# Building the second column half of the first matmul from seven half-size products, with operand sums made by accumulating DMA

## The chip, the cores and the metric

The kernel runs on one core of one Trainium2 chip. The metric is the device time of one execution in microseconds (us). A run more than 1.5% above the fastest of its kernel counts as slow and is left out of ratios. The profile is one execution; its span is about 1.8 us shorter than the measured time of the same execution (before: 122.1 against 123.87).

## The reference

```python
m, k, n, p = 1024, 1024, 2048, 1024
h = a @ b                                   # float32, random normal inputs
h = 0.5*h*(1 + tanh(sqrt(2/pi)*(h + 0.044715*h**3)))
return h @ c
```

## The kernel before

Tiles hold h transposed: the first matmul puts 128 columns of b (stationary) against 512 rows of a (moving), sums over eight k tiles in one PSUM bank, and ScalarE writes the GELU. All 16 column tiles are done for the upper 512 rows of a, then for the lower 512.

```python
def mm1(t, h):
    p = ppool.tile([128, H], F32, name="ps")
    for k in range(KT):                                  # 8 matmuls
        nc.tensor.matmul(p, bt(k, t), aT[h][:, k, :], start=(k == 0), stop=(k == KT - 1))
    gelu(t, h, p)
# ... (upper rows, loads, transposes of a's lower rows)
for t in range(NT):                                      # lower rows
    mm1(t, 1)
    # ... sums of c and of h on VectorE, a few per tile
```

The second matmul is already built from seven products of half-size blocks instead of eight (the Winograd form). VectorE makes every sum that this needs:

```python
# t1 = c12 - c11;  t2 = c22 - t1;  t3 = c22 - c12;  s1 = h21 + h22;  s2 = s1 - h11;  s3 = h11 - h21
for j in R: p = bank(); prod(p, whole(h11), whole(c11), j); nc.scalar.activation(u2[j], p, AF.Copy)
for j in range(3): p = bank(); prod(p, whole(h12), whole(c21), j); combine(j, 0, p, u2[j])
# ... then s2 x t2, s3 x t3, s1 x t1, s2 x c22, h22 x t2, each four output tiles of eight matmuls,
#     s2 and t2 having been replaced by s4 = h12 - s2 and t4 = t2 - c21, and one last narrow tile
```

bf16 holds a, b and half of the operands; sums are float32r. Loads that cast go through GpSimd's DMA queue, plain ones and the stores through SyncE's.

Of the kernel before, what the change touches and what calls it, by code (L numbers as in the profile page):

```python
# [19 lines left out]
def kernel(ctx, tc, a, b, c, out):  # L20
    nc = tc.nc
# [8 lines left out]
    W0 = N0 * 128  # L30
    N1 = 4
    W1 = N1 * 128

# [9 lines left out]
    b0stage = ctx.enter_context(tc.tile_pool(name="b0stage", bufs=8))  # L43
# [9 lines left out]
    NH = NT // 2  # L53
    aT = [keep.tile([128, KT, H], BF16, name=f"aT{h}", tag=f"A{h}") for h in range(2)]
    WB = W0 + W1
    b_lo = keep.tile([128, KT, WB], BF16, name="b_lo", tag="B0")
    b_hi = keep.tile([128, KT, N - WB], BF16, name="b_hi", tag="B1")

    def bcols(k0, kn, n0, w):
        if n0 < WB:  # L60
            return b_lo[:, k0:k0 + kn, ds(n0, w)]
        return b_hi[:, k0:k0 + kn, ds(n0 - WB, w)]

    def bt(k, t):
        return bcols(k, 1, t * 128, 128)[:, 0, :]


    hq = [[keep.tile([128, NH, H], F32R if h else BF16, name=f"h{h}{g}") for g in range(2)]
          for h in range(2)]
# [19 lines left out]
    for mt in range(4):  # L89
        load_a0(mt, 2 if mt == 3 else 1)  # L90
# [38 lines left out]
    for mt in range(4):  # L129
        if mt < 3:  # L130
            ab.append(cast_a0(mt + 1))
        turn0(mt, ab[mt], (0,) if mt == 3 else (0, 1))
        if mt < 3:
            warm_up(3)
    cast_b0(0)
    for k in range(KT):
        if k + 1 < KT:
            cast_b0(k + 1)
        for t in range(N0):
            nc.tensor.matmul(ps[t], bt(k, t), aT[0][:, k, :],  # L140
                             start=(k == 0), stop=(k == KT - 1))
# [3 lines left out]
    def gelu(t, h, p):  # L145
        nc.scalar.activation(hq[h][t // NH][:, t % NH, :], p, AF.Gelu_apprx_tanh)  # L146

    for t in range(N0):
        gelu(t, 0, ps[t])


    def load_b(k0, kn, n0, w):
        nc.gpsimd.dma_start(out=bcols(k0, kn, n0, w), in_=bv[:, k0:k0 + kn, ds(n0, w)])

    ps = [(tpool if t < 2 else ppool).tile([128, H], F32, name="pt" if t < 2 else "ps")
          for t in range(N1)]
    for k in range(0, KT, 4):
        load_b(k, 4, W0, W1)
        for i in range(4):
            for t in range(N1):  # L160
                nc.tensor.matmul(ps[t], bt(k + i, N0 + t), aT[0][:, k + i, :],  # L161
                                 start=(k + i == 0), stop=(k + i == KT - 1))
    for t in range(N1):
        gelu(N0 + t, 0, ps[t])


    def mm1(t, h):
        p = ppool.tile([128, H], F32, name="ps")
        for k in range(KT):
            nc.tensor.matmul(p, bt(k, t), aT[h][:, k, :],  # L170
                             start=(k == 0), stop=(k == KT - 1))
        gelu(t, h, p)

    W2 = 384
    for n0 in range(W0 + W1, N, W2):
        for k in range(0, KT, 4):
            load_b(k, 4, n0, W2)

    a1 = []
    for j in range(4):  # L180
        st = abf.tile([128, K], BF16, name="ab1")
        nc.gpsimd.dma_start(out=st, in_=av[:, 4 + j, :])
        a1.append(st)

    def turn(j):
        ab = a1[j]
        pt = tpool.tile([128, KT, 128], BF16, name="pt")
        for k in range(KT):
            nc.tensor.transpose(pt[:, k, :], ab[:, ts(k, 128)], ident)  # L189
        nc.vector.tensor_copy(aT[1][:, :, ts(j, 128)], pt)  # L190

    for t in range(N0 + N1, NT):
        mm1(t, 0)
        if t == NT - 3:
            turn(0)
        if t == NT - 2:
            turn(1)
            turn(2)
            turn(3)
# [7 lines left out]
    (h11, h12), (h21, h22) = hq  # L207
    c11 = keep.tile([128, NH, H], BF16, name="c11")
    c21 = keep.tile([128, NH, H], BF16, name="c21")
    c22 = keep.tile([128, NH, H], F32R, name="c22")  # L210
    c12 = keep.tile([128, NH, H], BF16, name="c12", tag="A0")
# [5 lines left out]
    load_c(c11, 0, 0)  # L217
    load_c(c22, 1, 1)
    load_c(c21, 1, 0)
    load_c(c12, 0, 1)  # L220

    t1 = [astage.tile([128, 2, H], F32R, name="t1", tag="a_st") for _ in range(4)]
# [150 lines left out]
```

## Time and profile before

| | before |
|---|---|
| time, median | 123.75 us (123.52 to 124.07) |
| span of the profile | 122.1 us |
| TensorE busy, VectorE busy | 116.1 us (95%), 64.6 us (53%) |
| chain that ended last | TensorE 88%, DMA 6% |
| second matmul starts, last matmul starts | 68.9 us, 119.0 us |

The page's strip chart has one digit for each fortieth of the span (9 is 90% or more). A line of the chain or of a timeline begins with start and length in us. The lines themselves are in the prediction below.

### The profile page before, as it was taken

To read this page: it belongs to the slowest core of one execution; us is meant where nothing else is said; L and a number is where in the kernel's file an instruction comes from. 1 tells how busy PE (TensorE), PEld (TensorE's weight loads), DVE (VectorE), ACT (ScalarE), POOL (GpSimd) and SP (SyncE) were. 2 spreads that over 40 slices of the span, in tenths; PEclk is the share of its full clock that TensorE was granted. 3 is DMA by queue.
4 is the path that set the end of the run, shared out by engine and by line. 5 is a ranking of instruction groups with operands and counts; after the bars stand their busy time and mean duration, and the time that the engine had idled before them with its cause. 6 is when DMAs were issued, how large, how long until landed. Compare 5 with 4: busy or idle time off the path is not lost.

```text
span 122.1 us, 1486 instructions
## 1 busy us (share of the span) xinstructions
PE 116.1 (95%) x577; PEld 68.3 (56%) x577; DVE 64.6 (53%) x95; ACT 30.7 (25%) x54; POOL 21.5 (18%) x26
## 2 busy tenths in 40 slices
PE   6977999999998999999999999999999999999990
PEld 2542444444456444444444444468888888888880
DVE  0352340000014200006999999999769999974351
ACT  4454752806331133233323331100000000000000
POOL 2000099132440220000000000797000000000000
PEclk9999999999999999999999999999999999999999
DMA  3999969999999999995000000000600022445425
GB/s 144 351 328 347 413 188 191 198 200 205 209 207 206 329 394 231 206 206 97 0 0 0 5 0 3 3 0 0 258 0 0 5 86 86 157 167 191 163 99 167
DMA packets 12582, 18.44 MB, mean 151 GB/s; under 512 B 800, under 2 KB 7584, under 8 KB 12576
## 3 DMA queue, kind: packets, MB, share of 16 engines
q0 software_dynamic: 7968, 8.91, 39.6%
q1 hardware_dynamic: 4464, 9.37, 20.9%
q10 hardware_dynamic: 144, 0.07, 0.2%
q8 instruction: 4, 0.07, 0.2%
q14 instruction: 2, 0.02, 0.0%
HBM read 20.97 MB, written 4.19 MB: 206 GB/s over the span
## 4 chain that ended last, share of the span: by engine, by line
PE 88%; DMA 6%; SPq 2%; DVE 1%; ACT 0%; issue 0%
PE ps L273 41%; PE ps L170 31%; PE ps L140 8%; DMA b_st<-in_b_dram 6%; PE ps L161 3%; PE pt L161 3%; SPq L78 2%; PE pt L189 1%; DVE aT L190 1%; ACT b_lo L126 0%; SPq L85 0%; DVE ot L342 0%; PE pt L115 0%
## 5 line engine op out<-in xcount | busy, mean ns | idle before, releaser
L146 ACT ACTIVATE h<-ps 128x512 fp32r<-128x512 f32 (+1 forms) x30 | 17.3, 602 | 28.6 <-PE ps L170 26.3
L170 PE MATMUL ps<-aT,b_hi 128*128 128x512 bf16 x96 | 21.4, 379 | 0.0
L170 PE MATMUL ps<-aT,b_lo 128*128 128x512 bf16 x80 | 17.4, 379 | 0.0
L170 PEld LDWEIGHTS <-b_hi 128*128 128x128 bf16 x96 | 9.3, 98 | 10.8
L273 PE MATMUL ps<-t,s 128*128 128x512 f32 x64 | 15.0, 392 | 0.0
L273 PE MATMUL ps<-t,h 128*128 128x512 f32 x64 | 14.8, 389 | 0.0
L273 PE MATMUL ps<-c,h 128*128 128x512 bf16 (+2 forms) x80 | 14.2, 336 | 0.0
L313 POOL COPY lk<-u 128x512 f32<-128x512 f32 x1 | 7.7, 7684 | 33.6 <-ACT u L306 33.6
L273 PEld LDWEIGHTS ps<-t,s 128*128 128x128 f32 x64 | 12.0, 188 | 2.6
L273 PEld LDWEIGHTS ps<-t,h 128*128 128x128 f32 x64 | 12.0, 188 | 2.5
L170 PEld LDWEIGHTS <-b_lo 128*128 128x128 bf16 x80 | 7.8, 98 | 9.4
L227 DVE TENSOR_TENSOR t<-c,c 128x1024 fp32r<-128x1024 bf16 x4 | 4.7, 1222 | 15.8 <-DMA c<-in_c_dram 15.7
L190 DVE COPY aT<-pt 128x1024 bf16<-128x1024 bf16 x4 | 2.7, 689 | 19.4 <-PE pt L189 19.3
L140 PE MATMUL ps<-aT,b_lo 128*128 128x512 bf16 x48 | 10.9, 380 | 0.8 <-DVE b_lo L125 0.8
L273 PEld LDWEIGHTS <-h 128*128 128x128 bf16 x80 | 7.2, 98 | 7.0 <-issue 0.3
L140 PEld LDWEIGHTS <-b_lo 128*128 128x128 bf16 x48 | 4.5, 98 | 6.6 <-DVE b_lo L125 1.1
L215 POOL DMA_DIRECT2D c<-in_c_dram x8 | 5.9, 744 | 11.7 <-PE ps L170 6.0
L296 DVE TENSOR_TENSOR ot<-ps,u 128x512 f32<-128x512 f32 x11 | 7.3, 684 | 1.1 <-PE ps L273 1.1
L101 PE MATMUL ps<-warm 128*128 128x512 bf16 x17 | 6.3, 516 | 1.2 <-DVE warm L49 1.2
L273 PE MATMUL ps<-c,s 128*128 128x512 f32 x32 | 7.4, 389 | 0.0
L273 PEld LDWEIGHTS ps<-c,s 128*128 128x128 f32 x32 | 6.0, 188 | 1.2
L125 DVE CAST b_lo<-b_st 128x384 bf16<-128x384 f32 x8 | 2.9, 368 | 5.1 <-DMA b_st<-in_b_dram 5.1
(40 smaller groups left out, 96.5 us busy)
## 6 DMA issues: line engine op xcount, KB each, us to landing
out_dram<-ot SPq DMA_DIRECT2D x15, 256.0 KB, 2.0
c<-in_c_dram POOLq DMA_DIRECT2D x6, 512.0 KB, 14.8
b_st<-in_b_dram SPq DMA_DIRECT2D x7, 384.0 KB, 8.1
c<-in_c_dram POOLq DMA_DIRECT2D x2, 1024.0 KB, 15.0
a_st<-in_a_dram SPq DMA_DIRECT2D x3, 512.0 KB, 4.1
b_hi<-in_b_dram POOLq DMA_DIRECT2D x4, 384.0 KB, 11.3
b_lo<-in_b_dram POOLq DMA_DIRECT2D x2, 512.0 KB, 7.2
ab<-in_a_dram POOLq DMA_DIRECT2D x4, 256.0 KB, 13.9
```

Source lines behind the costliest of these rows:

```text
L101: nc.tensor.matmul(ps[N0 - 1], warm[:, 0:128], warm, start=True, stop=True)
L125: nc.vector.tensor_copy(b_lo[:, k, 0:HW], b_st[k][:, 0:HW])
L140: nc.tensor.matmul(ps[t], bt(k, t), aT[0][:, k, :], start=(k == 0), stop=(k == KT - 1))
L146: nc.scalar.activation(hq[h][t // NH][:, t % NH, :], p, AF.Gelu_apprx_tanh)
L161: nc.tensor.matmul(ps[t], bt(k + i, N0 + t), aT[0][:, k + i, :], start=(k + i == 0), stop=(k + i == KT - 1))
L170: nc.tensor.matmul(p, bt(k, t), aT[h][:, k, :], start=(k == 0), stop=(k == KT - 1))
L190: nc.vector.tensor_copy(aT[1][:, :, ts(j, 128)], pt)
L215: nc.gpsimd.dma_start(out=dst[:, t:t + 4, :], in_=cv[:, r * NH + t:r * NH + t + 4, ts(q, H)])
L227: nc.vector.tensor_tensor(t1[i], c12[:, ts(i, 2), :], c11[:, ts(i, 2), :], op=SUB)
L273: nc.tensor.matmul(p, lhs(t)[:, ts(j, 128)], rhs(t)[:, q], start=(t == 0), stop=(t == NH - 1))
L296: nc.vector.tensor_tensor(ot, u if swap else p, p if swap else u, op=op)
L313: nc.gpsimd.tensor_copy(last_keep, last)
```

## The change

Output columns 1024 to 2047 of the first matmul (half of its 256 matmuls) become a two-by-two block product in the same seven-product form: 112 matmuls for 128. Its sums come on top of those that fill VectorE in the second matmul, so several, old and new, are made by accumulating DMA instead: the buffer holds a first term (for t2 and t3 ScalarE writes it there), and a transfer from GpSimd's queue adds the second. The core of the diff, with cuts marked by dots and the comments added here:

```diff
-    for t in range(N0 + N1, NT):
-        mm1(t, 0)
...
+    mm1(6, 0, h11[:, 6, :])
+    turn(0)
+    mm1(7, 0, h11[:, 7, :])
+    for j in (1, 2, 3):
+        turn(j)
... (as1, as2, as3, bt3, b12 in place, bt2: twelve sums on VectorE)
+    for t in range(NH):
+        mm1(t, 1, h21[:, t, :])
... (loads of c11, c12, c22)
+    for j in R:  # product 1, bf16
+        p = bank()
+        prod(p, KH, whole(bx), whole(aT[0]), j)
+        nc.scalar.activation(v2[:, j, :], p, AF.Copy)
+    for j in R:  # product 2, bf16
+        p = bank()
+        prod(p, KH, whole(bx, KH), whole(aT[0], KH), j)
+        add_gelu(h12[:, j, :], p, v2[:, j, :])
...
+    for j in R:  # product 3, float32r as all below
+        p = bank()
+        prod(p, KH, pairs(bt2), pairs(as2), j)
+        tt(v2[:, j, :], p, v2[:, j, :], op=ADD)
...
+    for i in range(2):
+        nc.gpsimd.dma_start(out=as2[i], in_=aT[0][:, P2[i + 2], :], accum_op=ADD)
+    for i in range(2):
+        nc.gpsimd.dma_start(out=bt2[i], in_=bx[:, P2[i + 2], :], accum_op=ADD)
... (product 4, bt3 and as3; product 5, b12 and as1)
+    c21 = keep.tile([128, NH, H], BF16, name="c21", tag="BX")
     load_c(c21, 1, 0)
...
+    for i in R:
+        nc.scalar.mul(t2[i], c22[:, P2[i], :], -1.0)
+        nc.gpsimd.dma_start(out=t2[i], in_=t1[:, P2[i], :], accum_op=ADD)
... (product 6, b22 and as2; product 7, bt2 and a22; s1 and s2 on VectorE; h11 x c11)
+    for i in R:
+        nc.scalar.mul(t3p(i), c12[:, P2[i], :], -1.0)
+        nc.gpsimd.dma_start(out=t3p(i), in_=c22[:, P2[i], :], accum_op=ADD)
... (h12 x c21, s3 on VectorE, s2 x t2)
-        sum_s4(i)
-        sum_t4(2 * j)
-        sum_t4(2 * j + 1)
+    for g in range(2):
+        nc.gpsimd.dma_start(out=s2[g], in_=h12[:, ts(g, KH), :], accum_op=ADD)
+    for i in R:
+        nc.gpsimd.dma_start(out=t2[i], in_=c21[:, P2[i], :], accum_op=ADD)
... (s3 x t3, s1 x t1, s2 x c22, h22 x t2, the narrow tile)
```

Line numbers in the profiles of the changed kernels are those of the changed files: L167 is `mm1`, L220 is `prod`, L285 the accumulates of t2, L339 and L340 t3's scaled copies and accumulates.

More of the change, by code (lines that the diff above doesn't have):

```diff
@@ L29 @@
     N0 = 6
-    W0 = N0 * 128
-    N1 = 4
-    W1 = N1 * 128
+    W0 = N // 2
+    KH = KT // 2
+    NH = NT // 2
+    R = range(4)
     av = a.rearrange("(mt p) k -> p mt k", p=128)
@@ L42 @@
     abf = ctx.enter_context(tc.tile_pool(name="abf", bufs=4))
-    b0stage = ctx.enter_context(tc.tile_pool(name="b0stage", bufs=8))
+    b0stage = ctx.enter_context(tc.tile_pool(name="b0stage", bufs=6))
     opool = ctx.enter_context(tc.tile_pool(name="opool", bufs=4))
@@ L51 @@
     make_identity(nc, ident)
-    NH = NT // 2
     aT = [keep.tile([128, KT, H], BF16, name=f"aT{h}", tag=f"A{h}") for h in range(2)]
-    WB = W0 + W1
-    b_lo = keep.tile([128, KT, WB], BF16, name="b_lo", tag="B0")
-    b_hi = keep.tile([128, KT, N - WB], BF16, name="b_hi", tag="B1")
-    def bcols(k0, kn, n0, w):
-        if n0 < WB:
-            return b_lo[:, k0:k0 + kn, ds(n0, w)]
-        return b_hi[:, k0:k0 + kn, ds(n0 - WB, w)]
-    def bt(k, t):
-        return bcols(k, 1, t * 128, 128)[:, 0, :]
-    hq = [[keep.tile([128, NH, H], F32R if h else BF16, name=f"h{h}{g}") for g in range(2)]
-          for h in range(2)]
+    a22 = keep.tile([128, KH, H], F32R, name="a22", tag="A22")
+    b_lo = keep.tile([128, KT, W0], BF16, name="b_lo", tag="B0")
+    bx = keep.tile([128, KT, H], BF16, name="bx", tag="BX")
+    b12 = keep.tile([128, KH, H], F32R, name="b12", tag="BT")
+    b22 = keep.tile([128, KH, H], F32R, name="b22", tag="BR")
+    (h11, h12), (h21, h22) = [[keep.tile([128, NH, H], F32R if h else BF16, name=f"h{h}{g}")
+                               for g in range(2)] for h in range(2)]
     a_st, b_st = {}, {}
@@ L88 @@
     gate = consts.tile([128, 1], F32, name="gate")
-    for mt in range(4):
+    for mt in R:
         load_a0(mt, 2 if mt == 3 else 1)
@@ L128 @@
     ab = [cast_a0(0)]
-    for mt in range(4):
+    for mt in R:
         if mt < 3:
@@ L139 @@
         for t in range(N0):
-            nc.tensor.matmul(ps[t], bt(k, t), aT[0][:, k, :],
+            nc.tensor.matmul(ps[t], b_lo[:, k, ts(t, 128)], aT[0][:, k, :],
                              start=(k == 0), stop=(k == KT - 1))
@@ L143, with gelu, bank @@
             turn0(3, ab[3], (1,))
-    def gelu(t, h, p):
-        nc.scalar.activation(hq[h][t // NH][:, t % NH, :], p, AF.Gelu_apprx_tanh)
+    def gelu(dst, src):
+        nc.scalar.activation(dst, src, AF.Gelu_apprx_tanh)
+    def bank(w=H):
+        return ppool.tile([128, w], F32, name="ps", padded_shape=[128, H])
     for t in range(N0):
-        gelu(t, 0, ps[t])
-    def load_b(k0, kn, n0, w):
-        nc.gpsimd.dma_start(out=bcols(k0, kn, n0, w), in_=bv[:, k0:k0 + kn, ds(n0, w)])
-    ps = [(tpool if t < 2 else ppool).tile([128, H], F32, name="pt" if t < 2 else "ps")
-          for t in range(N1)]
-    for k in range(0, KT, 4):
-        load_b(k, 4, W0, W1)
-        for i in range(4):
-            for t in range(N1):
-                nc.tensor.matmul(ps[t], bt(k + i, N0 + t), aT[0][:, k + i, :],
-                                 start=(k + i == 0), stop=(k + i == KT - 1))
-    for t in range(N1):
-        gelu(N0 + t, 0, ps[t])
-    def mm1(t, h):
-        p = ppool.tile([128, H], F32, name="ps")
-        for k in range(KT):
-            nc.tensor.matmul(p, bt(k, t), aT[h][:, k, :],
-                             start=(k == 0), stop=(k == KT - 1))
-        gelu(t, h, p)
-    W2 = 384
-    for n0 in range(W0 + W1, N, W2):
-        for k in range(0, KT, 4):
-            load_b(k, 4, n0, W2)
+        gelu(h11[:, t, :], ps[t])
     a1 = []
-    for j in range(4):
+    for j in R:
         st = abf.tile([128, K], BF16, name="ab1")
@@ L183 @@
         a1.append(st)
+    nc.gpsimd.dma_start(out=b12, in_=bv[:, 0:KH, W0 + H:N])
+    nc.gpsimd.dma_start(out=b22, in_=bv[:, KH:KT, W0 + H:N])
+    for k in range(0, KT, KH):
+        nc.gpsimd.dma_start(out=bx[:, k:k + KH, :], in_=bv[:, k:k + KH, W0:W0 + H])
     def turn(j):
-        ab = a1[j]
         pt = tpool.tile([128, KT, 128], BF16, name="pt")
         for k in range(KT):
-            nc.tensor.transpose(pt[:, k, :], ab[:, ts(k, 128)], ident)
+            nc.tensor.transpose(pt[:, k, :], a1[j][:, ts(k, 128)], ident)
@@ L190, in turn, with mm1 @@
         nc.vector.tensor_copy(aT[1][:, :, ts(j, 128)], pt)
-    for t in range(N0 + N1, NT):
-        mm1(t, 0)
-        if t == NT - 3:
-            turn(0)
-        if t == NT - 2:
-            turn(1)
-            turn(2)
-            turn(3)
-    (h11, h12), (h21, h22) = hq
+        nc.scalar.activation(a22[:, :, ts(j, 128)], aT[1][:, KH:KT, ts(j, 128)], AF.Copy)
+    def mm1(t, h, dst):
+        p = bank()
+        for k in range(KT):
+            nc.tensor.matmul(p, b_lo[:, k, ts(t, 128)], aT[h][:, k, :],
+                             start=(k == 0), stop=(k == KT - 1))
+        gelu(dst, p)
@@ new lines, with two @@
+    mm1(6, 0, h11[:, 6, :])
[3 more added lines that the diff above has]
+        turn(j)
+    tt = nc.vector.tensor_tensor
+    def two(pool, name, tag):
+        return [pool.tile([128, 2, H], F32R, name=name, tag=tag) for _ in range(2)]
+    as1 = two(astage, "as1", "a_st")
+    as3 = two(astage, "as3", "a_st")
+    bt3 = two(b0stage, "bt3", "b0_st")
+    as2 = two(b0stage, "as2", "b0_st")
+    bt2 = two(b0stage, "bt2", "b0_st")
+    P2 = [slice(2 * i, 2 * i + 2) for i in range(4)]
@@ new lines @@
+    for i in range(2):
+        tt(as1[i], aT[1][:, P2[i], :], aT[1][:, P2[i + 2], :], op=ADD)
+    for i in range(2):
+        tt(as2[i], aT[0][:, P2[i], :], as1[i], op=SUB)
+    for i in range(2):
+        tt(as3[i], aT[0][:, P2[i], :], aT[1][:, P2[i], :], op=SUB)
+    for i in range(2):
+        tt(bt3[i], b22[:, P2[i], :], b12[:, P2[i], :], op=SUB)
+    for i in range(2):
+        tt(b12[:, P2[i], :], b12[:, P2[i], :], bx[:, P2[i], :], op=SUB)
+    for i in range(2):
+        tt(bt2[i], b12[:, P2[i], :], b22[:, P2[i], :], op=SUB)
@@ new lines, with whole, pairs, prod @@
+    for t in range(NH):
+        mm1(t, 1, h21[:, t, :])
+    def whole(x, t0=0):
+        return lambda t: x[:, t0 + t, :]
+    def pairs(x):
+        return lambda t: x[t // 2][:, t % 2, :]
+    def prod(p, n, lhs, rhs, j, q=slice(0, H)):
+        for t in range(n):
+            nc.tensor.matmul(p, lhs(t)[:, ts(j, 128)], rhs(t)[:, q],
+                             start=(t == 0), stop=(t == n - 1))
+    def new_out():
+        return opool.tile([128, H], F32, name="ot")
+    def add_gelu(dst, p, u):
+        ot = new_out()
+        tt(ot, p, u, op=ADD)
+        gelu(dst, ot)
@@ L208 @@
     c11 = keep.tile([128, NH, H], BF16, name="c11")
-    c21 = keep.tile([128, NH, H], BF16, name="c21")
+    c12 = keep.tile([128, NH, H], BF16, name="c12")
     c22 = keep.tile([128, NH, H], F32R, name="c22")
-    c12 = keep.tile([128, NH, H], BF16, name="c12", tag="A0")
     def load_c(dst, r, q):
@@ L217 @@
     load_c(c11, 0, 0)
+    load_c(c12, 0, 1)
     load_c(c22, 1, 1)
-    load_c(c21, 1, 0)
-    load_c(c12, 0, 1)
-    t1 = [astage.tile([128, 2, H], F32R, name="t1", tag="a_st") for _ in range(4)]
-    t2 = [b0stage.tile([128, 1, H], F32R, name="t2", tag="b0_st") for _ in range(8)]
-    s1 = keep.tile([128, NH, H], F32R, name="s1")
-    def sum_t1(i):
-        nc.vector.tensor_tensor(t1[i], c12[:, ts(i, 2), :], c11[:, ts(i, 2), :], op=SUB)
-    def sum_t2(t):
-        nc.vector.tensor_tensor(t2[t], c22[:, t:t + 1, :], t1[t // 2][:, t % 2:t % 2 + 1, :], op=SUB)
@@ L232, in sum_s1 @@
-    def sum_s1(t):
-        nc.vector.tensor_tensor(s1[:, t, :], h21[:, t, :], h22[:, t, :], op=ADD)
-    for t in range(NT):
-        mm1(t, 1)
-        if 3 <= t < 7:
-            sum_t1(t - 3)
-        if 6 <= t < 10:
-            sum_t2(2 * (t - 6))
-            sum_t2(2 * (t - 6) + 1)
-        if t == WB // 128:
-            t3 = keep.tile([128, NH, H], F32R, name="t3", tag="B0")
-        if t >= NH + 1:
-            sum_s1(t - NH - 1)
-        if WB // 128 <= t < WB // 128 + 4:
-            i = t - WB // 128
-            nc.vector.tensor_tensor(t3[:, ts(i, 2), :], c22[:, ts(i, 2), :], c12[:, ts(i, 2), :], op=SUB)
@@ L249 @@
-    sum_s1(NH - 1)
-    s2 = [keep.tile([128, NH // 2, H], F32R, name=f"s2{g}", tag=f"A{g}") for g in range(2)]
-    def pair(x, i):
-        return x[i // 2][:, ts(i % 2, 2), :]
-    for i in range(4):
-        nc.vector.tensor_tensor(pair(s2, i), s1[:, ts(i, 2), :], h11[:, ts(i, 2), :], op=SUB)
-    for i in range(4):
-        nc.vector.tensor_tensor(h21[:, ts(i, 2), :], h11[:, ts(i, 2), :], h21[:, ts(i, 2), :], op=SUB)
-    s3 = h21
-    def sum_s4(i):
-        nc.vector.tensor_tensor(pair(s2, i), h12[:, ts(i, 2), :], pair(s2, i), op=SUB)
@@ L265, in sum_t4 @@
-    def sum_t4(t):
-        nc.vector.tensor_tensor(t2[t], t2[t], c21[:, t:t + 1, :], op=SUB)
-    def bank(w=H):
-        return ppool.tile([128, w], F32, name="ps", padded_shape=[128, H])
-    def prod(p, lhs, rhs, j, q=slice(0, H)):
-        for t in range(NH):
-            nc.tensor.matmul(p, lhs(t)[:, ts(j, 128)], rhs(t)[:, q],
-                             start=(t == 0), stop=(t == NH - 1))
-    def whole(x):
-        return lambda t: x[:, t, :]
+    v2 = keep.tile([128, 4, H], F32, name="v2", tag="A1")
@@ new lines, with sum_t1 @@
+    v3 = [abf.tile([128, H], F32, name="v3", tag="ab1") for _ in R]
+    t1 = keep.tile([128, NH, H], F32R, name="t1", tag="B0")
+    def sum_t1(i):
+        tt(t1[:, P2[i], :], c12[:, P2[i], :], c11[:, P2[i], :], op=SUB)
+    for j in R:
[6 more added lines that the diff above has]
+        add_gelu(h12[:, j, :], p, v2[:, j, :])
+        if j >= 2:
+            sum_t1(j - 2)
@@ new lines @@
+    for j in R:
+        p = bank()
+        prod(p, KH, pairs(bt2), pairs(as2), j)
+        tt(v2[:, j, :], p, v2[:, j, :], op=ADD)
+        if j >= 2:
+            sum_t1(j)
+    for i in range(2):
+        nc.gpsimd.dma_start(out=as2[i], in_=aT[0][:, P2[i + 2], :], accum_op=ADD)
+    for i in range(2):
+        nc.gpsimd.dma_start(out=bt2[i], in_=bx[:, P2[i + 2], :], accum_op=ADD)
+    for j in R:
+        p = bank()
+        prod(p, KH, pairs(bt3), pairs(as3), j)
+        tt(v3[j], p, v2[:, j, :], op=ADD)
@@ new lines @@
+    for j in R:
+        p = bank()
+        prod(p, KH, whole(b12), pairs(as1), j)
+        add_gelu(h22[:, 4 + j, :], p, v3[j])
+        tt(v2[:, j, :], p, v2[:, j, :], op=ADD)
+    c21 = keep.tile([128, NH, H], BF16, name="c21", tag="BX")
+    load_c(c21, 1, 0)
+    t2 = [astage.tile([128, 2, H], F32R, name="t2", tag="a_st") for _ in R]
+    for i in R:
+        nc.scalar.mul(t2[i], c22[:, P2[i], :], -1.0)
+        nc.gpsimd.dma_start(out=t2[i], in_=t1[:, P2[i], :], accum_op=ADD)
+    for j in R:
+        p = bank()
+        prod(p, KH, whole(b22), pairs(as2), j)
+        add_gelu(h12[:, 4 + j, :], p, v2[:, j, :])
@@ new lines, with sum_s1 @@
+    s1 = {}
+    def sum_s1(i):
+        s1[i] = b0stage.tile([128, 2, H], F32R, name="s1", tag="b0_st")
+        tt(s1[i], h21[:, P2[i], :], h22[:, P2[i], :], op=ADD)
+    sum_s1(2)
+    sum_s1(3)
+    for j in R:
+        p = bank()
+        prod(p, KH, pairs(bt2), whole(a22), j)
+        add_gelu(h22[:, j, :], p, v3[j])
+    sum_s1(0)
+    sum_s1(1)
+    s2 = [keep.tile([128, KH, H], F32R, name=f"s2{g}", tag=tag) for g, tag in ((0, "A0"), (1, "BR"))]
+    for i in (2, 3, 0, 1):
+        tt(s2[i // 2][:, P2[i % 2], :], h11[:, P2[i], :], s1[i], op=SUB)
@@ L279, in halves, with t3p, t3t @@
+    t3 = two(b0stage, "t3", "b0_st") + [keep.tile([128, KH, H], F32R, name="t3b", tag="BT")]
+    def t3p(i):
+        return t3[i] if i < 2 else t3[2][:, P2[i - 2], :]
+    def t3t(t):
+        return t3[t // 2][:, t % 2, :] if t < 4 else t3[2][:, t - 4, :]
     def halves(x):
         return lambda t: x[t // 4][:, t % 4, :]
-    def pairs(x):
-        return lambda t: x[t // 2][:, t % 2, :]
-    def ones(x):
-        return lambda t: x[t][:, 0, :]
-    def new_out():
-        return opool.tile([128, H], F32, name="ot")
@@ L291, in store, with combine @@
     def store(ot, m, q0, w=H, queue=nc.sync):
         queue.dma_start(out=out[ts(m, 128), ds(q0, w)], in_=ot[:, 0:w])
-    def combine(m, q, p, u, op=ADD, swap=False):
+    def combine(m, q, p, u):
         ot = new_out()
-        nc.vector.tensor_tensor(ot, u if swap else p, p if swap else u, op=op)
+        tt(ot, p, u, op=ADD)
         store(ot, m, q * H)
-    R = range(4)
-    u2 = [abf.tile([128, H], F32, name="u2", tag="ab1") for _ in R]
-    u3 = keep.tile([128, 4, H], F32, name="u3", tag="B1")
+    u2 = keep.tile([128, 4, H], F32, name="u2", tag="A22")
@@ L303 @@
+    u3 = [abf.tile([128, H], F32, name="u3", tag="ab1") for _ in R]
+    last = keep.tile([128, H], F32, name="last", tag="A1")
     for j in R:
         p = bank()
-        prod(p, whole(h11), whole(c11), j)
-        nc.scalar.activation(u2[j], p, AF.Copy)
+        prod(p, NH, whole(h11), whole(c11), j)
+        nc.scalar.activation(u2[:, j, :], p, AF.Copy)
+        if j == 3:
+            nc.scalar.activation(last, p, AF.Copy)
+    for i in R:
+        nc.scalar.mul(t3p(i), c12[:, P2[i], :], -1.0)
+        nc.gpsimd.dma_start(out=t3p(i), in_=c22[:, P2[i], :], accum_op=ADD)
@@ L307 @@
     for j in range(3):
         p = bank()
-        prod(p, whole(h12), whole(c21), j)
-        combine(j, 0, p, u2[j])
-    last = u2[3]
-    last_keep = opool.tile([128, H], F32, name="lk", bufs=1)
-    nc.gpsimd.tensor_copy(last_keep, last)
+        prod(p, NH, whole(h12), whole(c21), j)
+        combine(j, 0, p, u2[:, j, :])
+    for i in R:
+        tt(h21[:, P2[i], :], h11[:, P2[i], :], h21[:, P2[i], :], op=SUB)
+    s3 = h21
     for j in R:
         p = bank()
-        prod(p, halves(s2), ones(t2), j)
-        nc.vector.tensor_tensor(u2[j], p, u2[j], op=ADD)
+        prod(p, NH, halves(s2), pairs(t2), j)
+        tt(u2[:, j, :], p, u2[:, j, :], op=ADD)
@@ L318 @@
+    for g in range(2):
+        nc.gpsimd.dma_start(out=s2[g], in_=h12[:, ts(g, KH), :], accum_op=ADD)
+    for i in R:
+        nc.gpsimd.dma_start(out=t2[i], in_=c21[:, P2[i], :], accum_op=ADD)
     for j in R:
         p = bank()
-        prod(p, whole(s3), whole(t3), j)
-        nc.vector.tensor_tensor(u3[:, j, :], p, u2[j], op=ADD)
-        sum_s4(j)
+        prod(p, NH, whole(s3), t3t, j)
+        tt(u3[j], p, u2[:, j, :], op=ADD)
     for j in R:
         p = bank()
-        prod(p, whole(s1), pairs(t1), j)
@@ L326 @@
-        combine(4 + j, 1, p, u3[:, j, :])
-        nc.vector.tensor_tensor(u2[j], p, u2[j], op=ADD)
-        sum_t4(2 * j)
-        sum_t4(2 * j + 1)
+        prod(p, NH, pairs(s1), whole(t1), j)
+        combine(4 + j, 1, p, u3[j])
+        tt(u2[:, j, :], p, u2[:, j, :], op=ADD)
     for j in R:
         p = bank()
-        prod(p, halves(s2), whole(c22), j)
-        combine(j, 1, p, u2[j])
+        prod(p, NH, halves(s2), whole(c22), j)
+        combine(j, 1, p, u2[:, j, :])
     for j in R:
@@ L335 @@
         p = bank()
-        prod(p, whole(h22), ones(t2), j)
-        combine(4 + j, 0, p, u3[:, j, :], op=SUB, swap=True)
+        prod(p, NH, whole(h22), pairs(t2), j)
+        combine(4 + j, 0, p, u3[j])
     for q0, w, queue in ((0, 256, nc.sync), (256, 128, nc.scalar), (384, 128, nc.sync)):
         p = bank(w)
-        prod(p, whole(h12), whole(c21), 3, q=ds(q0, w))
+        prod(p, NH, whole(h12), whole(c21), 3, q=ds(q0, w))
         ot = new_out()
-        nc.vector.tensor_tensor(ot[:, 0:w], p, last_keep[:, ds(q0, w)], op=ADD)
+        tt(ot[:, 0:w], p, last[:, ds(q0, w)], op=ADD)
```

## The prediction

> **What bounds the kernel now.** I read the strip chart of the page first, then the chain that ended last in order of time, then the groups by shape, then the timeline of the first 20 us. The strip chart (40 slices of 3.05 us):
>
> ```profile
> PE   6977999999998999999999999999999999999990
> ...
> DVE  0352340000014200006999999999769999974351
> ...
> DMA  3999969999999999995000000000600022445425
> GB/s 144 351 328 347 413 188 191 198 200 205 209 207 206 329 394 231 206 206 97 0 0 0 5 0 3 3 0 0 258 0 0 5 86 86 157 167 191 163 99 167
> ```
>
> TensorE is full from 12 us to the end. VectorE is full only in the second half, where the second matmul is already built from seven products; from 18 to 54 us it is nearly idle. The DMA engines are nearly idle after 57 us. The chain says the same in time:
>
> ```profile
> 12.62 9.23 PE ps L140 x42
> ...
> 38.32 0.70 DVE aT L190
> 39.02 0.04 issue
> 39.06 0.61 PE pt L189 x8
> 39.67 29.35 PE ps L170 x136
> 69.02 50.17 PE ps L273 x240
> 119.20 0.02 issue
> 119.22 0.29 DVE ot L342
> ```
>
> Columns: start, length, what. After 12.6 us it is all TensorE, but for one wait of 0.74 us on the copy of a transposed tile. Only matmul time counts. A 512-column bf16 matmul costs 29.35/136 = 0.216 us. The second matmul has 160 matmuls of float32r, 56 full bf16 ones, 8 of half and 16 of quarter width (the last output tile): (50.17 - 56 x 0.216 - 8 x 0.108 - 16 x 0.054)/160 = 0.227 us for a float32r one, 0.011 us more than bf16. Other costs that I use, from the groups by shape:
>
> ```profile
> L227 DVE TENSOR_TENSOR t<-c,c 128x1024 fp32r<-128x1024 bf16 x4 | 4.7, 1222 | 15.8 <-DMA c<-in_c_dram 15.7
> ...
> L296 DVE TENSOR_TENSOR ot<-ps,u 128x512 f32<-128x512 f32 x11 | 7.3, 684 | 1.1 <-PE ps L273 1.1
> ...
> L190 DVE COPY aT<-pt 128x1024 bf16<-128x1024 bf16 x4 | 2.7, 689 | 19.4 <-PE pt L189 19.3
> ```
>
> A two-input sum takes 1.22 us for a pair of tiles, 0.68 us for one. The timeline of the start shows how fast slabs of b (384 KB each) arrive, by their casts:
>
> ```profile
> 16.07 0.52 ACT L126 ACTIVATE b_lo<-b_st 128x384 bf16<-128x384 f32 x1 [0.43 <-DMA b_st<-in_b_dram]
> ...
> 17.04 0.52 ACT L126 ACTIVATE b_lo<-b_st 128x384 bf16<-128x384 f32 x1 [0.44 <-DMA b_st<-in_b_dram]
> ...
> 18.01 0.52 ACT L126 ACTIVATE b_lo<-b_st 128x384 bf16<-128x384 f32 x1 [0.45 <-DMA b_st<-in_b_dram]
> ```
>
> One slab in 0.97 us (405 GB/s) against 6 x 0.216 = 1.30 us of matmuls: ahead of TensorE.
>
> **What the Trainium skill says.** "TensorE: Matmul & The Clock Gate", on the 56 ns gap, gives 215.7 ns for a warm 512-column matmul; the trace has 216. "DMA: Bandwidth & Descriptors", section SWDGE vs HWDGE vs iDMA: an accumulating DMA can only be issued from GpSimd; its rules add that later work on the same bytes must wait for the accumulate's semaphore. Nothing in this trace accumulates. "Collectives: The Full Stack", on the bandwidth ceiling: an add in the DMA engines is slower than a copy because it needs "two source reads", not because of the arithmetic. No page gives the rate of an accumulate from SBUF into SBUF. That is the number that decides this case.
>
> **The change part by part.**
> 1. Matmuls. Output columns 1024 to 2047 of the first matmul took 128 bf16 matmuls, 27.6 us. Now they take seven products of 16: two bf16 (32 x 0.216 = 6.9) and five float32r (80 x 0.227 = 18.2), 25.1 in all. **Gain 2.5 us.** The second matmul keeps its matmuls. So even a free change gives 2.0%, just at the limit of "faster".
> 2. Start. The slabs grow from 384 to 512 KB: 1.29 us each, equal to TensorE's 1.30. Taken from the second slab at 12.19 us, the eighth lands at 12.19 + 0.65 + 6 x 1.29 = 20.6; with 0.43 us of cast (the shape of a's casts) and 1.3 us of matmuls the stage ends near 22.3 instead of 21.85. **Loss 0.5 us**, some tenths more if the next loads from GpSimd overlap.
> 3. Transposes of the second half of a. Three now stand directly ahead of the matmuls that read them all, with two PSUM buffers. The third waits for a copy (0.4 us idle), and the next matmul for two more copies (1.0), 1.4 against 0.74 before. **Loss 0.6 us.**
> 4. Sums for the first matmul: 12 on VectorE at 1.22 = 14.6 us, in the stretch of 64 bf16 matmuls (13.8 us) with 7 us more before the third product needs them. b is loaded by then: hidden. During the products VectorE has 4 sums of c (4.9 us) and about 24 PSUM adds (16.4) in 25 us: busy, and late by some 2 us in the fifth product, but six PSUM banks cover that.
> 5. ScalarE gains eight scaled copies of 128x1024 to prime the accumulates, about 1.05 us each (estimate: 0.63 us for 512 columns and 0.52 for 384 is 0.83 ns a column). They sit in its queue between the GELUs; I find no stall above 1 us.
> 6. Accumulating DMAs: as2 and bt2 (4 of 512 KB), t2 (4), t3 (4), s2 (2 of 1 MB), t2 again (4): 10 MB of float32 written in the second 65 us, where the DMA engines were idle.
>
> Without 6 the sum is -2.5 + 0.5 + 0.6 = -1.4, with some tenths for the queues of 4 and 5 about -1.1: 122.6 us.
>
> **Where the accumulates collide.** The chart shows about 205 GB/s landing while loads cast float32 to bf16: 410 GB/s read, as is the 405 above. If reading is the limit and an accumulate reads source and destination (estimate, from the Collectives page and this rate), 512 KB takes 1.9 us with a bf16 source (0.79 MB read) and 2.6 us with a float32 one (1.05 MB).
> My hand schedule: matmuls of the lower a rows start at 29.0, the seven products at 42.9, the third ends at 53.4. Only then may as2 and bt2 be accumulated. Issue takes 0.75 us each (loads of c now), with about 1.1 us to the first bytes: as2 is complete near 60, and the sixth product needs it at 60.7; bt2 near 64, needed at 64.3. The load of c21 goes into bx's memory and stands in GpSimd's queue behind bt2's accumulates: 2.9 us from completion to first bytes, 5.1 us of data, until 71. The accumulates of t2 stand behind c21 in the same queue: 4 x 2.6, done at 82, needed at 80.0. Those of t3 follow: done at 92, needed at 89.3. The last two groups have 14 us of slack each.
> The DMA chain sets the start of the product s3 x t3: 53.4 + 1.9 + 7.7 + 2.9 + 5.1 + 20.5 + 1.0 = 92.5. From there: product s3 x t3, three more (4 x 7.26 us), the narrow tile 1.8 and the store's tail 2.9: 33.7 us. Span 126.2, and 1.65 us more for the measured time, as now (123.75 against 122.1): 127.9. The latencies may be a microsecond too long, and some issues overlap; so about 127.
>
> **The rivals.**
> A. The accumulates run as fast as copies (write limit 410 GB/s, 1.3 us each) or overlap better than I think: all hidden, 122.3 to 123.5. For it: the products are ordered so that each accumulate has 7 us or more, as of somebody who measured. Against: the two reads.
> B. They are read-bound as worked out: waits of 2 to 5 us on TensorE ahead of s2 x t2 and s3 x t3, 125 to 129.
> C. They are slower than read-bound (short packets, read-modify-write latency, issue slowed beside a busy VectorE: the one 128x512 copy on GpSimd took 7.7 us in the full VectorE stretch). At 3 us and 2.4 us the same sum gives 133; at twice the time 150.
> D. VectorE or ScalarE becomes the bound: VectorE loses 8 + 8 + 8 sums to the DMA, so its second half is lighter than now; a microsecond at most.
>
> **Range and chances.** Faster by 2% means below 121.3, under the best sum of 122.6: 4%. Within 2% (to 126.2) needs A or the mild half of B: 42%. Slower is the rest of B and C: 54%. The middle is 127.0. The low end is A; the high end leaves out only an accumulate near half the read-bound rate.
>
> **What would show it.** Matmul groups of 112 in place of 128, 0.216 and 0.227 us each; first stage ending near 22.3; idle of 1.4 us by the transposes. In the chain of waits TensorE waiting on t2 and t3 (accumulates), with bt2 close. DMA activity from 54 to about 92 us without a gap. The landing times of the accumulates settle A, B, C. Wrong would be: t2 and t3 complete before their products; or long waits elsewhere, say GpSimd's issues held by a wait I did not follow.

## The result, and the profile after

| | before | changed |
|---|---|---|
| time, median | 123.75 us | 131.19 us (129.99 to 132.72) |
| its fast runs | all four | 129.99 and 130.12 (two of four) |
| span of the profile | 122.1 us | 128.2 us |
| second matmul starts | 68.9 us | 67.2 us |
| last narrow tile starts | 117.2 us | 123.4 us |

The ratio is 1.051 (95% interval 1.047 to 1.055): slower. A ratio here is the mean of one kernel's fast runs over that of the other's fast runs of the same rounds, so not quite the ratio of the medians. The four runs of the changed kernel lie 2.7 us apart; its two slow runs were not profiled and are not explained here.

The page's strip chart of the changed kernel, in slices of 3.2 us:

```profile
PE   6976999969999999999999999389839999999991
...
DVE  0343331279999139999999998962404447463351
...
PEclk9999999999999999999999999958999999999999
DMA  4999999999999999199489999999999999944334
GB/s 142 365 360 367 418 345 170 268 403 258 206 206 206 214 390 269 36 248 263 114 100 159 195 208 206 220 245 245 242 268 281 270 275 277 325 178 164 116 131 164
```

Before, TensorE's row was nines to the end and the DMA row had a hole from 57 us. Now the DMA row is full from 54 to 112 us but for a dip at 61 to 67 us, where c21's load waits for bt2's landing, and TensorE's has a hole from 80 to 96 us, with its clock down in two slices. VectorE has its own light stretch behind the same hole: it is not what TensorE waits for. The timeline of TensorE in that stretch says what is:

```profile
67.21 12.26 PE L220 MATMUL ps<-c,h 128*128 128x512 bf16 x54
79.12 1.27 PE L220 MATMUL ps<-t,s 128*128 128x512 f32 x4
80.93 0.73 PE L220 MATMUL ps<-t,s 128*128 128x512 f32 x2 [0.55 <-DMA t<-t]
83.79 7.77 PE L220 MATMUL ps<-t,s 128*128 128x512 f32 x26 [2.12 <-DMA t<-t]
91.39 1.07 PE L220 MATMUL ps<-t,h 128*128 128x512 f32 x4
93.13 0.70 PE L220 MATMUL ps<-t3b,h 128*128 128x512 f32 x2 [0.68 <-DMA t3b<-c]
95.61 0.70 PE L220 MATMUL ps<-t3b,h 128*128 128x512 f32 x2 [1.77 <-DMA t3b<-c]
96.15 1.09 PE L220 MATMUL ps<-t,h 128*128 128x512 f32 x4
...
101.63 7.42 PE L220 MATMUL ps<-t,s 128*128 128x512 f32 x32
```

The bracket gives the idle time before the line and what ended it. The second matmul starts 1.7 us earlier than before (67.2 for 68.9). Then s2 x t2 takes 12.3 us (79.1 to 91.4) and s3 x t3 10.2 us (91.4 to 101.6), 22.5 together, where the kernel before took 14.7 (80.8 to 95.5): 7.8 us lost (8.0 against 64 matmuls without a gap). 7.8 - 1.7 = 6.1, the difference of the spans. After 101.6 nothing is lost. The end of the chain that ended last is the same fact:

```profile
79.48 15.99 DMA t3b<-c
95.48 0.14 issue
95.61 29.74 PE ps L220 x146
125.35 0.02 issue
125.37 0.29 DVE ot L377
```

Before, the chain ended in 50 us of TensorE without a break; now what came before the last 30 us is a transfer.

In the trace each transfer on GpSimd's queue posts 16 increments of its semaphore. The core has 16 DMA engines; that each posts one increment is a reading, since the trace does not name them. Here are the first and last times (us). The last is what a waiting engine sees: TensorE goes on at 83.79 and 95.61, just behind 83.7 and 95.5. The columns after the first belong to the experiments below; "product order" is the run with that product moved alone, "best" the one with one transposed block earlier.

```
last transfer of      changed         copies          memory swap     product order   best
bt2 accumulate      62.6 - 63.0     63.3 - 63.7     63.5 - 63.9     60.0 - 61.0     59.1 - 60.1
c21 load            72.1 - 72.6     72.8 - 73.5     69.7 - 72.3     69.3 - 69.6     68.0 - 68.8
t2 accumulate       82.1 - 83.7     78.0 - 79.7     79.7 - 83.3     79.2 - 80.7     77.9 - 79.3
t3 accumulate       94.2 - 95.5     85.6 - 86.6     91.8 - 95.5     91.8 - 93.0     84.1 - 85.0
```

### The profile page after: what moved, and what is told of

Read it like the earlier page. It is cut to its first block, busy times and chain, and to the rows that moved or that the text cites. A ratio compares the mean times of both kernels' runs of the same rounds, so it can differ in the third digit from the quotient of the medians.

```text
span 128.2 us, 1539 instructions
## 1 busy us (share of the span) xinstructions
PE 115.9 (90%) x555; PEld 74.5 (58%) x561; DVE 77.3 (60%) x107; ACT 44.1 (34%) x71; POOL 28.3 (22%) x41
## 4 chain that ended last, share of the span: by engine, by line
issue 37%; DMA 28%; PE 23%; POOL 9%; POOLq 0%; DVE 0%
PE ps L220 23%; DMA t3b<-c 12%; DMA bx<-in_b_dram 10%; DMA bt<-bx 6%; POOL t L285 2%; POOL ab L150 2%; POOL t L340 1%; POOL c L238 1%; POOL t3b L340 1%; POOL b L152 1%; POOL b L153 1%; POOL gate L86 0%; DVE ot L377 0%; POOL ident masks.py:199 0%; POOL ident masks.py:197 0%
## 5 line engine op out<-in xcount | busy, mean ns | idle before, releaser
L220 PE MATMUL ps<-t,s 128*128 128x512 f32 x64 | 17.2, 425 | 2.7 <-DMA t<-t 2.7
L167 PE MATMUL ps<-aT,b_lo 128*128 128x512 bf16 x77 | 17.6, 379 | 0.9 <-DVE aT L161 0.8
L325 DVE TENSOR_TENSOR ot<-ps,u 128x512 f32<-128x512 f32 x15 | 10.2, 690 | 11.8 <-PE ps L220 9.7
L220 PEld LDWEIGHTS ps<-t,s 128*128 128x128 f32 x64 | 13.0, 207 | 6.4 <-DMA t<-t 3.5
L220 PE MATMUL ps<-c,h 128*128 128x512 bf16 (+2 forms) x78 | 14.1, 336 | 0.1
L138 ACT ACTIVATE h<-ot 128x512 bf16<-128x512 f32 (+1 forms) x16 | 9.3, 622 | 12.5 <-DVE ot L228 12.5
L167 PEld LDWEIGHTS <-b_lo 128*128 128x128 bf16 x80 | 7.7, 98 | 9.9 <-DVE aT L161 1.0
L228 DVE TENSOR_TENSOR ot<-ps,v 128x512 f32<-128x512 f32 x16 | 10.4, 682 | 5.0 <-PE ps L220 5.0
L138 ACT ACTIVATE h<-ps 128x512 bf16<-128x512 f32 (+1 forms) x16 | 8.9, 606 | 10.1 <-PE ps L167 9.6
L220 PE MATMUL ps<-t,h 128*128 128x512 f32 x48 | 11.7, 389 | 0.0
L220 PEld LDWEIGHTS <-h 128*128 128x128 bf16 x80 | 7.1, 98 | 7.0 <-issue 0.5
L220 PEld LDWEIGHTS ps<-t,h 128*128 128x128 f32 x48 | 9.0, 188 | 1.9
L220 PE MATMUL ps<-as,bt 128*128 128x512 f32 x32 | 7.6, 396 | 0.0
L220 PE MATMUL ps<-c,s 128*128 128x512 f32 x32 | 7.4, 389 | 0.0
L220 PE MATMUL ps<-as,b 128*128 128x512 f32 x32 | 7.4, 389 | 0.0
L117 DVE CAST b_lo<-b_st 128x512 bf16<-128x512 f32 x8 | 3.4, 426 | 6.5 <-DMA b_st<-in_b_dram 6.5
L220 PE MATMUL ps<-aT,bx 128*128 128x512 bf16 x32 | 7.1, 379 | 0.0
```

Source lines behind the costliest of these rows:

```text
L117: nc.vector.tensor_copy(b_lo[:, k, 0:HW], b_st[k][:, 0:HW])
L138: nc.scalar.activation(dst, src, AF.Gelu_apprx_tanh)
L167: nc.tensor.matmul(p, b_lo[:, k, ts(t, 128)], aT[h][:, k, :], start=(k == 0), stop=(k == KT - 1))
L220: nc.tensor.matmul(p, lhs(t)[:, ts(j, 128)], rhs(t)[:, q], start=(t == 0), stop=(t == n - 1))
L228: tt(ot, p, u, op=ADD)
L325: tt(ot, p, u, op=ADD)
```

## The experiments

The theory: TensorE waits at the end of one chain of transfers (as2, bt2, c21, t2, t3, in this order on one queue), whose rate is set by reading two streams for every sum. Rivals: latency and place in the queue rather than the rate; the half clock after a wait; VectorE or ScalarE as the real bound. Each experiment starts from the changed kernel unless it says otherwise. Ratios are to the kernel before, from the same rounds. The changed kernel itself was not run again in those rounds, and its profile started well: its first stage ended at 21.6 us, in the profiles of the experiments at 21.7 to 22.7. So a difference of about 1 us from its 130.0 shows nothing.

### Plain copies in place of the accumulates of t2 and t3 (wrong result)

```diff
-nc.gpsimd.dma_start(out=t2[i], in_=t1[:, P2[i], :], accum_op=ADD)
+nc.gpsimd.dma_start(out=t2[i], in_=t1[:, P2[i], :])
-nc.gpsimd.dma_start(out=t3p(i), in_=c22[:, P2[i], :], accum_op=ADD)
+nc.gpsimd.dma_start(out=t3p(i), in_=c22[:, P2[i], :])
```

> The eight accumulates of t2 and t3 become plain copies of the same size from the same sources, same queue, same order (wrong result on purpose: only the second read, of the destination, goes away). Theory (an accumulate is bound by reading two float32 streams, 2.5 us for 512 KB): a copy should take about 1.3 us, t2 and t3 are then complete before their products, the 8.0 us that the two products lost go, and the time falls from 130.0 to about 122 us (121.5 to 123). Rival (place in the queue, issue and latency of GpSimd's transfers, not their rate): no more than 1 to 2 us are won, 128 or more.

Measured: 122.83 us (122.19 to 123.33), ratio 0.990 (0.985 to 0.995). The result is wrong, as meant. TensorE has no wait left in this stretch:

```profile
79.84 7.63 PE L220 MATMUL ps<-t,s 128*128 128x512 f32 x32
87.31 1.07 PE L220 MATMUL ps<-t,h 128*128 128x512 f32 x4
```

The four copies of t2 land 1.27 us apart (first increments at 74.17, 75.44, 76.72, 77.98), the four accumulates 2.48 us apart (74.64, 77.10, 79.59, 82.07), with the same sources, bytes written, packet size (4096 bytes), queue and order. The ratio is 1.95. The run takes the addition away together with the read of the destination, so it does not separate these two. For the read speaks that the accumulates from a bf16 source add and write as many elements and yet take 2.0 us, and that the bytes read, if the destination counts, come out nearly alike (estimates: 1.05 MB in 2.48 us is 423 GB/s, 0.79 MB in 2.0 us 393, 0.52 MB in 1.27 us 413). The copies' speed-up decides against a rival of latency or order alone, and since all of VectorE's and ScalarE's work was still there, against those two as the bound. 122.8 us is what the change costs with t2's and t3's transfers at copy speed.

### c21 in other memory

```diff
-c21 = keep.tile([128, NH, H], BF16, name="c21", tag="BX")
+c21 = keep.tile([128, NH, H], BF16, name="c21", tag="BT")
-t3 = ... keep.tile([128, KH, H], F32R, name="t3b", tag="BT")
+t3 = ... keep.tile([128, KH, H], F32R, name="t3b", tag="BX")
```

> c21 goes into the memory of b12 (free after the fifth product) and t3b into that of bx, so the load of c21 no longer waits for the accumulates of bt2 to land; nothing else changes. Theory (one chain of transfers on GpSimd's queue, c21's place in it costing a bubble of some 3 us): c21 and t2 come about 3 us earlier, t2 lands near 80.5 instead of 83.8, t3 near 91.8 instead of 95.6; time 126 to 127 us. Rival (the rate of the accumulates alone, the bubble being filled by waiting data anyway): 129 to 130.

Measured: 131.25 us (130.97 to 132.03), ratio 1.060: a miss. In the table above the first of the 16 increments for t2 comes 2.4 us earlier (79.7 for 82.1), but the last only 0.4 us earlier: it is 3.7 us behind the first. For t3 the last is where it was, 95.5. Two things hide part of its worth. The products of this run start 0.9 us later (43.0 for 42.1), so counted from there t2's last landing is 1.3 us earlier and t3's 0.9. And the clock is at half from 95.1 to 98.5 us, at t3's landing, so that 31.1 us of TensorE follow it instead of 29.7. The bubble ahead of c21 was real; of the expected 3 us the last landings show about 1. The Trainium skill ("DMA: Bandwidth & Descriptors", section Latency and other measured facts) says that two of the engines are usually slower than the others, and gives a cause only as a guess; the trace agrees that a few increments lag, but does not name their engines. For t2's last transfer in the changed kernel 15 increments come from 82.1 to 82.6 us and one at 83.7; here three trail. The lag of that transfer is 3.5 and 3.7 us in the two profiles in which c21's load is issued before bt2's accumulates have landed (this one and the one without the early product order), and 1.2 to 1.9 us in the ten others. Why is not tested.

### Idle matmuls ahead of s2 x t2

```diff
     combine(j, 0, p, u2[:, j, :])
+pw = tpool.tile([128, H], F32, name="pt")
+for _ in range(12): nc.tensor.matmul(pw, warm[:, 0:128], warm, start=True, stop=True)
```

> Twelve idle matmuls (2.6 us) on a spare PSUM bank stand ahead of the product of s2 and t2, where TensorE waits for t2 and then runs 3.4 us at half clock. Theory (t3's last accumulate lands at 95.6 whatever TensorE does, and the rest follows from it): the half-clock stretch ahead of t3 goes away, but TensorE only waits longer for t3; time unchanged within 0.5 us of 130.0, or worse where the wait for t3 brings the half clock there. Rival (the half clock is worth its 1.7 us): 128.3.

Measured: 133.22 us (132.39 to 133.68), ratio 1.074, the worse branch of the theory. The half-clock stretch at 83.8 to 87.3 us is gone, and another one of 6.8 us stands at 95.4, where TensorE waits for t3:

```profile
94.30 0.71 PE L220 MATMUL ps<-t3b,h 128*128 128x512 f32 x2 [2.14 <-DMA t3b<-c]
96.81 1.19 PE L220 MATMUL ps<-t3b,h 128*128 128x512 f32 x2 [1.81 <-DMA t3b<-c]
97.81 1.91 PE L220 MATMUL ps<-t,h 128*128 128x512 f32 x4
```

Four matmuls take 1.91 us from issue to end instead of 1.07. A half-clock stretch ahead of t3's landing costs nothing, since TensorE would wait anyway; of one that falls behind it, half the length is lost. Here t3 lands at 96.7 us and 5.5 us of the stretch lie behind that; half of them, 2.8, is about what is lost: 35.2 us follow the landing to the end of the span, instead of 32.7. The landing itself is 1.2 us later than in the changed kernel's profile, but the products of this run also began 1.1 us later.

### t3 on VectorE

```diff
-for i in R:
-    nc.scalar.mul(t3p(i), c12[:, P2[i], :], -1.0)
-    nc.gpsimd.dma_start(out=t3p(i), in_=c22[:, P2[i], :], accum_op=ADD)
 s3 = h21
+for i in R: tt(t3p(i), c22[:, P2[i], :], c12[:, P2[i], :], op=SUB)
```

> t3 is summed on VectorE (4 x 1.22 us after s3's sums) instead of ScalarE's scaled copies and four accumulates; a right result. Theory: VectorE finishes t3 near 89.7, before the product of s2 and t2 ends (91.4), so the 3.0 us of waiting for t3 go and those for t2 stay; time about 127. Rival (VectorE is the bound once it is given anything back): the product of s3 and t3 starts later than 95.6, time 130 or more.

Measured: 127.70 us (126.32 to 128.12), ratio 1.028 (1.021 to 1.035). As expected: no wait for t3, and the chain now passes through the last landing of t2, at 84.2 us. The profiled run is the fastest of the four, at a clock of 0.996; the others, 1.0 to 1.8 us longer, have 0.982 to 0.986.

### The product of bt2 and as2 moved from third to second place

This lets as2 and bt2 be accumulated earlier, while the DMA engines were idle (the GB/s row of the chart has 36 in one slice). The names v2 and v3 change places behind it; no sum is added. The edit in outline:

```diff
 product 1
-product 2                      # bx x a, upper k
 product 3                      # bt2 x as2, now into v3
 accumulates of as2 and bt2
+product 2
 products 4 to 7
```

> The product of bt2 and as2 moves ahead of the one of bx and a's lower columns, so as2 and bt2 can be accumulated 3.5 us earlier, in the 3 us in which the DMA engines stand idle behind the loads of c; same matmuls, same sums, same bytes. Theory (TensorE waits for one chain of read-bound transfers that begins with as2): every later landing moves forward by 2 to 3 us, t2's last from 83.7 to about 81, t3's last from 95.5 to about 92.5 to 93.5; the half clock at t2 may vanish; time 126.5 to 128. Rival (the last of the 16 engines sets the landings and has its own pace, as the exchange of c21's memory suggested): under 1 us, 129 to 130.

Measured: 130.10 us (129.22 to 130.44), ratio 1.050: a miss in time, while the landings moved as expected (table: t2 80.7 for 83.7, t3 93.0 for 95.5) and s2 x t2 ran without a wait. Busy time by stretch in this run, with the granted clock as the third number from the right:

```profile
87.40:93.20 5.80, 1.83 (x8) 0.92 (x7) 0.74 (x2) 0.00 (x0) 4.84 (x6) 0.86 1.08 248
93.20:97.00 3.80, 3.80 (x9) 3.06 (x10) 0.69 (x1) 0.00 (x0) 0.00 (x0) 0.50 1.04 274
97.00:101.60 4.60, 4.60 (x18) 3.70 (x18) 1.38 (x2) 0.00 (x0) 0.00 (x0) 0.85 1.01 260
```

One long wait for t3 has taken the place of two short ones, and the clock is at half from 91.6 to 98.4 us. From t3's landing to the start of the last vector sum it takes 32.3 us, against 29.9 in the changed kernel: the 2.5 us by which t3 landed earlier are given back there.

### The same with idle matmuls ahead of s3 x t3

```diff
+pw = tpool.tile([128, H], F32, name="pt")
+for _ in range(18): nc.tensor.matmul(pw, warm[:, 0:128], warm, start=True, stop=True)
 for j in R: p = bank(); prod(p, NH, whole(s3), t3t, j)
```

> The kernel with the product of bt2 and as2 moved forward (130.1 us, t3's last landing at 93.0, then 6.8 us at half clock), with 18 idle matmuls (3.9 us) where TensorE waits for t3. Theory (the 2.5 us that the earlier chain won were given back as half clock after one long wait): the half-clock stretch goes or falls to one of 3.4 us, t3 still lands near 93, and from there to the last matmul it takes about 30 us as in the changed kernel instead of 32.2; time about 127.5 to 128.5. Rival (the clock is no part of it): 130.

Measured: 127.62 us (127.08 to 127.78), ratio 1.030 (1.027 to 1.034), as expected; the profiled run's mean clock is 1.0. The end of its chain:

```profile
80.49 12.81 DMA t3b<-c
93.30 0.14 issue
93.44 29.71 PE ps L220 x146
```

t3 lands at the same time, and 29.7 us follow instead of 32.2. So the half clock is worth 2.5 us here, and what remains (127.6) is the wait itself.

### Earlier product order, c21's other memory, and t3 half and half

Two of t3's four pairs stay with the accumulating DMA, the other two go to VectorE behind s3.

```diff
 # product order and memory of c21 and t3b as in the runs above
-for i in R:
+for i in (0, 1):
     nc.scalar.mul(t3p(i), c12[:, P2[i], :], -1.0)
     nc.gpsimd.dma_start(out=t3p(i), in_=c22[:, P2[i], :], accum_op=ADD)
 s3 = h21
+for i in (2, 3): tt(t3p(i), c22[:, P2[i], :], c12[:, P2[i], :], op=SUB)
```

> That order, c21 in the memory of b12, and of t3's four pairs two by accumulating DMA and two by VectorE after s3. Theory: as2 and bt2 land near 60, c21 near 66.5, t2 near 77 to 80 (needed at 79.1), t3's two accumulates near 82 to 84, VectorE's two pairs at 87.2 (needed at 87.3): hardly a wait left on TensorE, 122 to 123 us, below the kernel before by about 1%. Rival (an engine that lags keeps t2 near 83 whatever the order): 125 to 127.

Measured: 122.88 us (122.70 to 123.57), ratio 0.994 (0.991 to 0.996), a right result. TensorE has no wait from the first product to the end:

```profile
29.25 13.99 PE ps L167 x64
43.23 75.30 PE ps L220 x352
118.54 0.02 issue
118.56 0.29 DVE ot L379
```

### The same with t3 wholly on VectorE

> As the run before, but t3 wholly on VectorE. Theory: VectorE reaches t3's end only at 89.7, 2 us after the product of s2 and t2, so TensorE waits 2 to 3 us there, for VectorE this time: 124.5 to 125.5 us. If VectorE has slack, it equals the run before.

Measured: 124.88 us (124.73 to 125.10), ratio 1.009. As expected, the wait comes back and is VectorE's:

```profile
89.02 0.73 PE L220 MATMUL ps<-t3b,h 128*128 128x512 f32 x2 [0.40 <-DVE t3b L346]
90.16 0.73 PE L220 MATMUL ps<-t3b,h 128*128 128x512 f32 x2 [0.40 <-DVE t3b L346]
```

In this order neither the DMA engines nor VectorE make t3 in time alone; each can make half.

### One transposed block earlier, on top of the half-and-half version

```diff
 turn(0)
+turn(1)
 mm1(7, 0, h11[:, 7, :])
-for j in (1, 2, 3): turn(j)
+for j in (2, 3): turn(j)
```

> The best version so far (122.9 us), with the second transposed block of a's lower rows moved ahead of the last matmul group of the upper rows, so that fewer copies stand between the transposes and the matmuls that read them. Theory (the prediction's term of 0.6 us for the transposes): the wait of 0.3 us for a PSUM buffer goes and the one of 0.8 us for the last copy becomes shorter or stays; 122.2 to 122.7 us. If the load of that block of a comes too late, no gain.

Measured: 122.39 us (122.24 to 122.66), ratio 0.989 (0.986 to 0.992). This is the best version: 1.1% below the kernel before, with a right result; that is less than the 2% that count as faster here, but its interval leaves out 1. The wait for a PSUM buffer is gone; one of 0.94 us for the last copy stays.

### The best version less one part each

> The best version (122.4 us) with c21 back in bx's memory, where its load waits for bt2's accumulates to land instead of for the fifth product. Theory: with the earlier product order both come at about the same moment (bt2 lands at 61, the fifth product ends near 61), so the exchange is worth nothing here: 122.2 to 122.8. If it is needed, t2 comes some 2 us later and TensorE waits: 124 or more.

Measured: 122.68 us (122.50 to 123.07), ratio 0.992 (0.987 to 0.997): the exchange of memory is worth nothing that these runs can show.

> The best version with the product of bt2 and as2 back in third place. Theory (the chain must begin early enough for t2): t2's last landing goes back to about 83, 3 us or more after TensorE wants it, with or without a half-clock stretch: 124.5 to 127. If t3's half on VectorE was all that mattered: 122.2 to 123.

Measured: 124.45 us (124.06 to 125.04), ratio 1.007, a hair under the expected range. TensorE waits 1.64 us for t2, whose last increment is at 82.9 us, and the clock does not fall. So the product order is needed; t3's half alone is not enough.

## Why the prediction was right

The prediction said slower, with 127.0 us as the middle, 122.3 to 123.5 (rival A) as the low end and a high end short of its 150; measured were 131.2 as the median and 130.0 for the fast runs. It gave "slower" only 54%, so being right about that was partly luck. The place and kind of the wait were right: TensorE waits for t2 and t3 at the end of the chain of accumulates. The loss was 3.3 us in the prediction and 6.3 in the fast runs. By its steps:

- **Matmuls, a gain of 2.5 us.** Right. The seven products run from 42.14 to 67.21 us, 25.1 us as predicted.
- **Start, a loss of 0.5 us.** Too large for the profiled run, where the first stage ended at 21.6 us and not at 22.3; about right over all profiles, where it ended between 21.6 and 22.7, mostly at 22.3 to 22.6. It varies by about a microsecond from run to run.
- **Transposes, a loss of 0.6 us.** About right: waits of 0.33 and 0.79 us stand there, 1.1 for the predicted 1.4, against 0.74 before. The run with one block earlier won 0.5 us of median (122.39 for 122.88, in different rounds, so hardly clear of noise).
- **VectorE and ScalarE hidden.** Right. The sums of the fifth product end at 63.9 us, some 4 us after it, and TensorE did not wait. ScalarE's scaled copies take 1.05 us, as estimated.
- **Accumulates read-bound.** The sizes were right: 2.48 us for a float32 source (predicted 2.6), 2.0 us for a bf16 source (first increments at 56.53, 58.65, 60.64, 62.60; predicted 1.9), 1.27 for a copy. They fit two reads; that the addition itself costs nothing is not shown. Rival A fails. Of rival C only the direction holds (130.0 is over B's 129): the accumulates on their own were about as fast as worked out. (Its 150 is a slip: at twice the time the prediction's own sum, 127.9 + 20.5 + 7.7, gives 156.)
- **The chain's end.** This is the term that was mis-sized: 95.5 us for 92.5. In the prediction's sum the chain stands at 63.0 (bt2), 71.0 (c21), 81.3 (t2) and 91.5 (t3), and 1.0 us of latency ends it. Measured were 63.0 for bt2's last increment, then 72.1, 82.1 and 94.2 for the first ones, and 1.3 us more for t3's last. So c21's load took 9.1 us instead of 8.0, t2 10.0 instead of 10.3, t3 12.1 instead of 10.3. Of c21's 1.1 us, 1.0 lie in its second half. t3's accumulates come 3.2, 3.2 and 2.7 us apart instead of 2.6, while three stores of 256 KB move beside them and take 10.6 us (median) to land instead of about 2. The sizes agree: t3's four exceed t2's by 2.1 us, and three stores at the copy's 413 GB/s would need 1.9 (estimate). With t3 wholly on VectorE the same stores land 2.0 to 2.2 us after their issue. That the stores delay t3 fits this, but no run leaves them out.
- **What follows the chain.** 33.7 us were predicted from the start of s3 x t3. In the profile t3's last pair lands at 95.5 and 32.7 us remain: 1.0 us less, as most of the first output tile was done by then. The 3.0 us of the chain less this 1.0 put the span at 128.2 for 126.2; the prediction had also rounded its sum of 127.9 down to 127.
- **What would show it.** The prediction expected DMA activity from 54 us without a gap; there is one, at 61 to 67 us, which its own 2.9 us between bt2 and c21 implied.
- **The half clock.** Not foreseen at all. In the profiled run it cost nothing, since it fell ahead of t3's landing; where it fell behind, as with the product order alone, it cost 2.5 us.

Two things stay open: why the second half of c21's load took 3.5 to 3.8 us in the changed kernel and the runs that keep its order and memory, 2.8 to 2.9 with c21 in other memory alone or with t3 in halves, and 2.5 to 2.7 with the early product order; and which engine lags, and why.

## What to carry to other kernels

An idle DMA engine is not free adding capacity: size an accumulate by the bytes of its source and destination both, which fitted here, and follow its whole queue to the instruction that waits. When one resource cannot make an operand in time, split the operand between two resources that each have time for half. And where a wait of some microseconds on TensorE can't be avoided, look at the clock after it, because a gain ahead of the wait can be paid back there.

## What the Trainium skill lacked or had wrong

- "DMA: Bandwidth & Descriptors" has no rate for an accumulate. Here, SBUF to SBUF, 512 KB of float32 written took 2.48 us with a float32 source (211 GB/s landed), 2.0 us with a bf16 source (262 GB/s), and 1.27 us as a plain copy (413 GB/s).
- "Collectives: The Full Stack" (the bandwidth ceiling) explains a slower add by two reads, for transfers between cores, with a ratio of 1.93. Within one core's SBUF the ratio here is alike, 2.48/1.27 = 1.95; that the second read is the cause there too fits, but was not separated from the addition.
- "TensorE: Matmul & The Clock Gate" (What's actually happening) has the clock fall to half after an idle window of about 3.4 us. Here it fell at 83.8 us, when two matmuls (0.45 us) had run within the 3.4 us before; a wait of 1.6 us elsewhere did not bring it. The stretches were 3.4 or 6.8 us long. The page does not say that such a stretch can be free, as it was ahead of t3's landing.
- "DMA: Bandwidth & Descriptors" (Latency and other measured facts) says that some engines are usually slower, without a size. Here the last of the 16 increments of one accumulate came 0.25 to 4.5 us after the first, and that took away most of what c21's other memory won.
